# The u blocks of a gated mixer as seven products of half-width matmuls

## The chip, the cores and the metric

The kernel runs on one core of a Trainium2 chip. The metric is the device time of one execution in microseconds (us): for the kernel before, the median of three runs, 2037.05 us (2037.03 to 2038.43). A core has a matmul engine, TensorE (PE; its loads of the stationary operand are shown as PEld), a vector engine, VectorE (DVE), ScalarE for activation functions (ACT), GpSimd (POOL) and SyncE (SP). SP and POOL issue the DMAs.

## The reference

Two layers act on x of 512 tokens by 1024 features, float32. Each layer is a SwiGLU half step, a mixer and a second SwiGLU half step, each with a layer norm behind it. The change is in the mixer's input projection, in the part called u:

```
zq, zf, zi, zg, zu, zv, za, zb = jnp.split(x @ w_in, IN_SPLITS, axis=-1)
...
u = jax.nn.gelu(zu)
v = layer_norm(jax.nn.gelu(zv), sg_ln_g, sg_ln_b)
...
mixed = jnp.einsum('gts,bnsgc->bntgc', ws, v) + sg_bs.T[None, None, :, :, None]
y_b = (u * mixed.reshape(B, T, SG_WIDTH)) @ w_branch_b
```

zu has 512 features, that is, 4 blocks of 128; the sum behind each runs over 1024 features, that is, 8 row tiles of 128.

## The kernel before, in words

**Split operands.** Every large product is made in three terms. An operand is split into a high part (copied by ACT with rounding to the matmul's float32 form, line 126) and a low part (the difference, DVE, line 127), and high x high, high x low and low x high are summed in PSUM.

**Plain blocks.** features(name) takes the next block of w_in from the iterator blk: weights() issues one DMA of 512 KB into a "raw" buffer (line 132, SP's queue) and splits it into two "w" buffers; proj() (line 155) runs 8 row tiles x 3 terms = 24 matmuls of 128 x 128 weights against 512 tokens into one PSUM bank. There are 4 raw buffers (NRAW), 10 w buffers (NW) and 3 "sa" buffers for evictions (NSA).

**Seven products.** Several stages use a scheme for a 2 x 2 product of blocks with seven products instead of eight. In the first product of the SwiGLU (seven_pairs, matmuls at line 590) a unit is a pair of features j and j + 11 of both halves of the weights; tokens and the summed rows are each cut in two halves. The operands of the seven products are, by ORDER: a, t, c, b, a, d, c on the weights' side, where t = a + b, b = d + b, a = a + b and c = a + c are formed in the raw buffers by DVE (sum(), line 570) before the split, and A11, s1, A12, s3, s2, s4, A22 on the side of x. The sums s1 to s4 of x are made by x_sums(). One product is 2 blocks x 4 row tiles x 3 terms = 24 matmuls against 256 tokens, so a pair has 168. PairWeights loads a, b, c and d (two DMAs of 256 KB each), and the split of a weight is written AHEAD = 3 products before its use. The results lie in four banks, A, B, C and E; evictions() takes them out and combines them behind each product.

i and v of the mixer use another form of the scheme (class Seven, two_tokens, matmuls at line 366): there the sums of the weights are formed in DRAM by accumulating DMAs on POOL's queue (sums_in_dram, line 307), and two_b(k), two_c(k), two_d(k) load and split them. two_b(k) makes the weights B11 and t1 (one split), and for even k those of t2 for two k (another split).

**Order of the mixer.** The queries and gates f and q of four heads; the g blocks, four calls of features() with a Sigmoid on ACT (line 1050) and a product on DVE (line 1051) behind each; the u blocks, four calls of features() with a GELU behind each (line 1063); then i and v by two_tokens(); then the gates z and what follows. x_sums (s_task) and sums_in_dram (in_dram) are side tasks, and so are the scores of each head (head_scores: small matmuls sp, lv, lx at lines 892, 953, 963, with DVE work between them) and the outputs of the heads. A hand-written planner (class Flow) keeps a clock of estimated PE time; each tick of a proj() or product() adds the estimated cost, and writes at most one step of a side task that has come due into the program at that place. flow.finish(task) writes all that is left of a task.

**Order of the instructions.** The order on each engine is laid down when the program is built, by the order in which instructions are written and the estimated readiness of their inputs and buffers. An instruction passed through pin() while pinned[0] is true stays behind the one written before it on its engine; the others may be placed earlier or later. seven_pairs() and the loads, sums and splits of its weights are written under pinned[0]; the matmuls themselves, features(), two_tokens() and head_scores() are not.

Of the kernel before, what the change touches and what calls it, by code (L numbers as in the profile page):

```python
# [28 lines left out]
F32 = mybir.dt.float32  # L29
F32R = mybir.dt.float32r  # L30
I32 = mybir.dt.int32
AF = mybir.ActivationFunctionType
ALU = mybir.AluOpType
AX = mybir.AxisListType

P = 128
D = 1024
T = 512
DEPTH = 2
DFF = 2816  # L40
NF = DFF // P
# [42 lines left out]
def trunk(ctx: ExitStack, tc, x_in, xt_in, w13, w2, w_in, w_iv, w_br, w_out, ln_g, ln_b, lb_in, hgn, sgg, sgb, sgws,  # L84
          sgbs, masks, tril_in, ident_in, out):
    nc = tc.nc
    V, S, G, PE = nc.vector, nc.scalar, nc.gpsimd, nc.tensor
# [3 lines left out]
    wk = ctx.enter_context(tc.tile_pool(name="wk", bufs=1))  # L91
# [11 lines left out]
    def slot(name, dtype=F32):  # L103
        return big.tile([P, 2, 512], dtype, tag="h", name=name, bufs=NS)
# [13 lines left out]
    pinned = [False]  # L118

    def pin(ins):  # L120

        if pinned[0]:
            tc.keep_in_program_order(ins)
# [21 lines left out]
    NS, NRAW, NSA = 34, 4, 3  # L145
# [130 lines left out]
    NH2 = NF // 2  # L276
# [257 lines left out]
    AHEAD = 3  # L534

    class PairWeights:
# [25 lines left out]
        def split(self):  # L562
# [2 lines left out]
            split(hi, lo, getattr(self, src))  # L565
            self.parts.append((hi, lo))

        def sum(self, to, u, v):
            to, u, v = (getattr(self, n) for n in (to, u, v))
            pin(V.tensor_tensor(to, u, v, op=ALU.add))  # L570

    def seven_pairs(seven, s, ks, weights_of, first, due):


        half = slice(0, 256), slice(256, 512)
        movs = {"A11": lambda m: (xh[m // 2][:, m % 2, half[0]], xl[m // 2][:, m % 2, half[0]]),
                "A12": lambda m: (xh[2 + m // 2][:, m % 2, half[0]], xl[2 + m // 2][:, m % 2, half[0]]),
                "A22": lambda m: (xh[2 + m // 2][:, m % 2, half[1]], xl[2 + m // 2][:, m % 2, half[1]])}
        for c in s:
            movs[c] = lambda m, c=c: (s[c][0][:, m], s[c][1][:, m])  # L580

        def product(ps, units, c, first):
            for z in range(2):
                hi, lo = units[0][:, z], units[1][:, z]
                for m in range(4):
                    ms = slice(m * P, (m + 1) * P)
                    mh, ml = movs[c](m)
                    for i, (a, v) in enumerate(((hi, mh), (hi, ml), (lo, mh))):
                        start = first and z == 0 and m == 0 and i == 0
                        PE.matmul(ps[:, half[z]], a[:, ms], v, start=start, stop=(m == 3 and i == 2),  # L590
                                  skip_group_check=not (first and z == 0))
                    flow.tick(3 * 120.0)

        pws = {ks[0]: first}
        at = lambda n: (ks[n // 7], n % 7)
        last = 7 * len(ks)
        banks = {}

        def evictions(k, m):
            b, r = banks[k], seven.room(k).rearrange("p q t -> p (q t)")  # L600
            lower, upper = r[:, 0:512], r[:, 512:1024]
            if m == 0:
                pin(S.activation(upper, b["A"], AF.Copy))
            elif m == 2:
                pin(S.activation(lower, b["A"], AF.Silu))
            elif m == 1:
                b["b1"] = wk.tile([P, T], F32, tag="sa", name="b1", bufs=NSA)
                pin(S.activation(b["b1"], b["C"], AF.Copy))
            elif m == 3:
                pin(V.tensor_tensor(b["b1"], b["b1"], b["E"], op=ALU.subtract))  # L610
            elif m == 4:
                pin(V.tensor_tensor(upper, upper, b["B"], op=ALU.subtract))
                pin(V.tensor_tensor(b["b1"], b["b1"], upper, op=ALU.subtract))
            elif m == 5:
                b0 = wk.tile([P, T], F32, tag="sa", name="b0", bufs=NSA)
                pin(V.tensor_tensor(b0, b["C"], upper, op=ALU.subtract))
                pin(V.tensor_tensor(lower, lower, b0, op=ALU.mult))
            elif m == 6:
                pin(V.tensor_tensor(upper, b["E"], upper, op=ALU.add))
                yield  # L620
                pin(S.activation(upper, upper, AF.Silu))
                pin(V.tensor_tensor(upper, upper, b["b1"], op=ALU.mult))

        for n in range(last):
            k, m = at(n)
            nk = at(n + 7)[0] if n + 7 < last else None
            if m == 0 and nk is not None:
                pws[nk] = weights_of(nk)
                pws[nk].load_d()
            elif m == 1 and nk is not None:  # L630
                pws[nk].load_c()
            ev = evictions(*at(n - 1)) if n else iter(())
            next(ev, None)
            if m == 0:
                banks[k] = {c: bank(f"f{c}{k}") for c in "ABCE"}
                pws[k].sum("a", "a", "b")
            elif m == 1:
                pws[k].sum("c", "a", "c")
            elif m == 2 and nk is not None:
                pws[nk].sum("t", "a", "b")  # L640
            elif m == 3 and nk is not None:
                pws[nk].sum("b", "d", "b")
            if n + AHEAD < last:
                pws[at(n + AHEAD)[0]].split()
            for _ in ev:
                pass
            if m == 3:
                for v in due.get(k, ()):
                    seven.activation_sums(v)
            c, mov, _ = ORDER[m]  # L650
            product(banks[k][c], pws[k].parts[m], mov, c == "B" or m in (0, 1, 3))
        for _ in evictions(*at(last - 1)):
            pass

    FRONT = [10]
# [6 lines left out]
    def ffn(l, i, first, next_weights):  # L662
        last = next_weights is None

        front = FRONT
        by_seven = [k for k in range(NH2) if k not in front]
        order = by_seven[0:2] + front + by_seven[2:]
        seven = Seven(lambda k: w2[l, i, k], order, front + by_seven[3:5])
# [26 lines left out]
        s = {}  # L695
        bufs = []
# [4 lines left out]
        def first_weights():  # L701
            pinned[0] = True
            bufs.extend(slot(f"r{v}") for v in ("t", "c0", "c1"))
            pw = weights_of(by_seven[0])
            pw.load_c()
            pw.load_d()
            pw.sum("t", "a", "b")
            for _ in range(AHEAD):
                pw.split()
            pw.sum("b", "d", "b")  # L710
            pinned[0] = False
            return pw

        if first is None:
# [8 lines left out]
            pw = first_weights()  # L723
            plain(js[1], second)
        else:
            first = [blocks(j, w) for j, w in zip(js, first)]
# [5 lines left out]
            for z, j in enumerate(js):  # L732
                pair_of(j, first[z], 256, 256)
                glu(j, first[z])
                if z == 0:
                    pw = first_weights()
        flow.finish(s_task)
        seven.home[by_seven[2]] = (xl[0][:, 0, 256:512], xl[0][:, 1, 256:512], xh[0][:, :, 256:512], xh[1][:, :, 256:512])

        hold = small("hold")  # L740
# [1 line left out]
                                                 op0=ALU.mult, op1=ALU.add))  # L742
        in_dram = flow.add(seven.sums_in_dram(order))
        pinned[0] = True
        seven_pairs(seven, s, by_seven, weights_of, pw, dict(zip((1, 2, 4, 5, 7, 8), ([v] for v in front + by_seven[0:5]))))
        pinned[0] = False
        flow.finish(in_dram)
        return seven.run(0.5 / ALPHA, (l, 2 * i), last, by_seven[5:], next_weights)
# [24 lines left out]

    T_AT = {2: 0, 4: 256, 8: 384, 16: 448, 32: 480, 64: 496, 128: 504}

    def mixer_weights(l):
        return [weights(w_in[l, b], f"{'fq'[b % 2]}{b // 2}", True) for b in range(4)]

    def mixer(l, lb, om, first, next_weights):
# [4 lines left out]
        hg = wk.tile([P, NH], F32, tag="hg", name="hg", bufs=1)  # L784
        nc.gpsimd.dma_start(hg, hgn[l])

        blk = iter(range(4, 32))
        s = {}
        seven = Seven(lambda k: w_iv[l, k], list(range(KT // 2)), [])

        def features(name):
            w = weights(w_in[l, next(blk)], name)
            ps = bank(name)
            proj(ps, w, 0, from_x)
            return ps

        def two_tokens():

            ks, ops, mm = seven.order, seven.ops, seven.mm
# [7 lines left out]
            A, B, C = ([bank(f"{v}{tt}") for tt in range(2)] for v in ("iA", "iB", "iC"))  # L807
            u, p5 = (wk.tile([P, 2, 512], F32, tag="rs", name=v, bufs=2) for v in ("iu", "ip5"))
            for i, k in enumerate(ks):
                seven.two_b(k)  # L810
                if i < len(ks) - 2:
                    for ps, p in ((A, P1), (B, P6), (C, P5)):
                        for tt in range(2):
                            mm(ps, p, [k], tt, True, True)
# [35 lines left out]
        gate, qk, raw, sc = [], [], [], []  # L850
# [194 lines left out]

        gs = [slot(f"gs{i}") for i in range(2)]
        for h in range(NH):
            ps = features(f"g{h}")
            sl = gs[h // 2][:, h % 2, :]
            S.activation(sl, ps, AF.Sigmoid)  # L1050
            V.scalar_tensor_tensor(sl, ps, hg[:, h:h + 1], sl, op0=ALU.mult, op1=ALU.mult)
# [5 lines left out]
                yield from head_out(h)  # L1057


        u = [slot(f"u{i}") for i in range(2)]  # L1060
        for j in range(4):
            ps = features(f"u{j}")
            S.activation(u[j // 2][:, j % 2, :], ps, AF.Gelu_apprx_tanh)
        flow.finish(s_task)
        flow.finish(in_dram)
        two_tokens()
        late.append(flow.add(all_out(), 4000.0))
        cst = slot("cst")
# [39 lines left out]
        z = [[], []]  # L1108
# [177 lines left out]
```

## Time and profile before

| | |
|---|---|
| median of 3 runs | 2037.05 us (2037.03 to 2038.43) |
| profiled execution, time | 2035.33 us |
| profiled execution, span | 2033.5 us |
| mean granted TensorE clock | 0.998 of full |
| busy: PE, PEld | 2022.2, 1840.6 us |
| busy: DVE, ACT, POOL | 1639.4, 996.8, 370.5 us |
| u blocks, layer 0 | from 430.1 to 453.2 us of the span |
| u blocks, layer 1 | from 1440.7 to 1463.8 us of the span |

The profile is one execution on the chip. Busy times are sums over an engine's instructions; "idle before" in the groups and timelines is the time in which the engine had nothing running, with what ended it. Matmuls overlap each other, so the distance between starts, not the duration, is the pace. Names such as u<-xh,h_u give the tile written and the tiles read; L155 is line 155 of the kernel.

### The profile page before, as it was taken

The numbers are of one execution on the slowest core, as the hardware profiler recorded it, in microseconds if no ns is written. First come the engines' busy times: TensorE is split into PE (matmuls) and PEld (weight loads), VectorE is DVE, ScalarE is ACT, GpSimd is POOL, SyncE is SP. The second block draws the span as 40 slices with busy tenths as digits, with TensorE's granted clock in tenths as the row PEclk, the third lists the DMA queues.
The fourth block names the chain that finished last, engine by engine and source line by source line (L and its number), as shares of the span: only waits on it lengthen the run. The fifth ranks groups of instructions, "written<-read, shape, count | busy, mean of one in ns | idle before, by whom it ended". The sixth has DMA issues, their size and how long they took to land. (4 is left out here: it accounts for less than half of the span.)

```text
span 2033.5 us, 33362 instructions
## 1 busy us (share of the span) xinstructions
PE 2022.2 (99%) x12880; PEld 1840.6 (91%) x12880; DVE 1639.4 (81%) x2453; ACT 996.8 (49%) x1438; POOL 370.5 (18%) x478
## 2 busy tenths in 40 slices
PE   9999999999999999999999999999999999999998
PEld 8999988888888999998899999898888889999986
DVE  8999988956436799999789999889564467999986
ACT  6544665336323554556555456662353235444563
POOL 2322002301000143210132320032010002323101
PEclk9999999999999999999999999999999999999999
DMA  6999777735243289988649997776352433999873
GB/s 233 257 258 238 239 253 238 153 110 181 83 154 115 105 234 241 226 258 269 203 153 271 253 243 242 256 231 137 118 175 83 145 114 113 255 239 230 264 258 129
DMA packets 167550, 404.60 MB, mean 199 GB/s; under 512 B 18880, under 2 KB 19008, under 8 KB 167392
## 3 DMA queue, kind: packets, MB, share of 16 engines
q1 hardware_dynamic: 113472, 261.22, 38.2%
q0 software_dynamic: 53920, 141.26, 29.5%
q8 instruction: 101, 1.65, 0.3%
q14 instruction: 57, 0.47, 0.1%
HBM read 380.38 MB, written 131.07 MB: 252 GB/s over the span
## 5 line engine op out<-in xcount | busy, mean ns | idle before, releaser
L307 POOL DMA_DIRECT2D t<-in_w_dram x176 | 145.5, 901 | 219.5 <-DMA t<-in_w_dram 103.1
L127 DVE TENSOR_TENSOR l_pc<-rc,h_pc 128x1024 fp32r<-128x1024 f32 x80 | 97.8, 1222 | 19.0 <-ACT h_pc L126 19.0
L307 POOL DMA_DIRECT2D t<-t x104 | 56.7, 545 | 288.2 <-DMA t<-in_w_dram 258.6
L155 PE MATMUL z<-xh,h_z 128*128 128x512 f32 x256 | 103.2, 403 | 0.0
L155 PE MATMUL z<-xh,l_z 128*128 128x512 f32 x256 | 99.9, 390 | 0.0
L155 PE MATMUL z<-xl,h_z 128*128 128x512 f32 x256 | 99.9, 390 | 0.0
L127 DVE TENSOR_TENSOR l_pa<-ra,h_pa 128x1024 fp32r<-128x1024 f32 x80 | 97.7, 1221 | 0.0
L126 ACT ACTIVATE h_pc<-rc 128x1024 fp32r<-128x1024 f32 x80 | 84.0, 1050 | 21.0 <-PE fB L590 20.0
L186 POOL TENSOR_SCALAR rstd<-ssq 128x1 f32<-128x1 f32 x24 | 19.3, 803 | 406.8 <-ACT sq L211 406.8
L590 PE MATMUL fA<-xh,h_pc 128*128 128x256 f32 x320 | 90.8, 284 | 0.1
L590 PE MATMUL fC<-xs1h,l_pt 128*128 128x256 f32 x320 | 90.7, 283 | 0.0
L590 PE MATMUL fB<-xs2l,h_pa 128*128 128x256 f32 x320 | 90.7, 283 | 0.0
L590 PE MATMUL fC<-xs1l,h_pt 128*128 128x256 f32 x320 | 90.7, 283 | 0.0
L590 PE MATMUL fB<-xs2h,h_pa 128*128 128x256 f32 x320 | 90.7, 283 | 0.0
L590 PE MATMUL fC<-xs4l,h_pd 128*128 128x256 f32 x320 | 90.7, 283 | 0.0
L590 PE MATMUL fE<-xs3l,h_pb 128*128 128x256 f32 x320 | 90.7, 283 | 0.0
L590 PE MATMUL fB<-xs2h,l_pa 128*128 128x256 f32 x320 | 90.7, 283 | 0.0
L590 PE MATMUL fE<-xh,l_pc 128*128 128x256 f32 x320 | 90.7, 283 | 0.0
L590 PE MATMUL fA<-xh,l_pa 128*128 128x256 f32 x320 | 90.7, 283 | 0.0
L590 PE MATMUL fC<-xs4h,l_pd 128*128 128x256 f32 x320 | 90.7, 283 | 0.0
L590 PE MATMUL fE<-xs3h,l_pb 128*128 128x256 f32 x320 | 90.7, 283 | 0.0
L590 PE MATMUL fC<-xs4h,h_pd 128*128 128x256 f32 x320 | 90.7, 283 | 0.0
(411 smaller groups left out, 7561.6 us busy)
## 6 DMA issues: line engine op xcount, KB each, us to landing
t<-in_w_dram POOLq DMA_DIRECT2D x88, 512.0 KB, 8.8
t<-t POOLq DMA_DIRECT2D x104, 256.0 KB, 5.5
r_d<-t SPq DMA_DIRECT2D x104, 256.0 KB, 4.2
t<-in_w_dram POOLq DMA_DIRECT2D x88, 256.0 KB, 7.1
r_c<-in_w_dram SPq DMA_DIRECT2D x44, 512.0 KB, 4.8
ra<-in_w_dram SPq DMA_DIRECT2D x80, 256.0 KB, 6.0
rb<-in_w_dram SPq DMA_DIRECT2D x80, 256.0 KB, 7.2
rc<-in_w_dram SPq DMA_DIRECT2D x80, 256.0 KB, 7.7
```

Of the source, the lines that this page charges most:

```text
L126: pin(S.activation(hi, src, AF.Copy))
L127: pin(V.tensor_tensor(lo, src, hi.bitcast(F32), op=ALU.subtract))
L155: PE.matmul(ps[:, n0:n0 + n], a[:, cs], m[:, n0:n0 + n], start=(i == 0), stop=(i == 3 * nk - 1))
L186: G.tensor_scalar(r, ssq, inv, eps, op0=ALU.mult, op1=ALU.add)
L307: tc.keep_in_program_order(nc.gpsimd.dma_start(*of(k), **kw))
L590: PE.matmul(ps[:, half[z]], a[:, ms], v, start=start, stop=(m == 3 and i == 2), skip_group_check=not (first and z == 0))
```

## The change

The four calls of features() for u are replaced by one pair of the seven-product scheme: seven_pairs() runs with one unit whose a and b are the blocks 0, 1 and 2, 3 of u for the first half of the rows, and c and d the same blocks for the second half. For this seven_pairs() no longer holds the SwiGLU's evictions and its work beside the products, but takes both as functions (evict, beside); the SwiGLU passes what it had. The opening of a first pair (loads of c and d, t = a + b, three splits, b = d + b) becomes PairWeights.begin(). In the mixer, the weights are loaded and begin() is written, pinned, before the weights of the third g block. The side tasks s_task and in_dram are finished before the u blocks instead of behind them. evict_u() takes two copies, four GELUs on ACT and five operations on DVE from the four banks. Beside products 4 and 5 the weights of i and v for k = 0 and 1 are loaded and split, pinned; two_tokens() leaves out what is there. t, a and b take raw buffers, c and d two buffers of tag "rs".

```diff
+        def begin(self):
+            self.load_c()
+            self.load_d()
+            self.sum("t", "a", "b")
+            for _ in range(AHEAD):
+                self.split()
+            self.sum("b", "d", "b")
...
-    def seven_pairs(seven, s, ks, weights_of, first, due):
+    def seven_pairs(s, ks, weights_of, first, evict, beside):
...
-            if m == 3:
-                for v in due.get(k, ()):
-                    seven.activation_sums(v)
+            beside(k, m)
...
+    U_AT = 12
...
-        blk = iter(range(4, 32))
+        blk = iter([*range(4, U_AT), *range(U_AT + 4, 32)])
...
             for i, k in enumerate(ks):
-                seven.two_b(k)
+                if ("B11", k) not in ops:
+                    seven.two_b(k)
...
         for h in range(NH):
+            if h == 2:
+                pinned[0] = True
+                t, c = (wk.tile([P, 2, 512], F32, tag=v, name=f"ru{v}", bufs=n) for v, n in (("raw", NRAW), ("rs", 2)))
+                pw = PairWeights(lambda j: w_in[l, U_AT + 2 * (j // NF) + j % NF // NH2], 0, t, c)
+                pw.begin()
+                pinned[0] = False
             ps = features(f"g{h}")
...
-        u = [slot(f"u{i}") for i in range(2)]
-        for j in range(4):
-            ps = features(f"u{j}")
-            S.activation(u[j // 2][:, j % 2, :], ps, AF.Gelu_apprx_tanh)
         flow.finish(s_task)
         flow.finish(in_dram)
+        u = [slot(f"u{i}") for i in range(2)]
+
+        def evict_u(k, m, b):
+
+            def gelu(i, half, v):
+                pin(S.activation(u[i][:, :, 256 * half:256 * half + 256], v.rearrange("p (z t) -> p z t", z=2),
+                                 AF.Gelu_apprx_tanh))
+
+            if m == 0:
+                b["u"] = wk.tile([P, T], F32, tag="sa", name="uu", bufs=NSA)
+                pin(S.activation(b["u"], b["A"], AF.Copy))
+            elif m == 1:
+                b["b1"] = wk.tile([P, T], F32, tag="sa", name="ub1", bufs=NSA)
+                pin(S.activation(b["b1"], b["C"], AF.Copy))
+            elif m == 2:
+                gelu(0, 0, b["A"])
+            elif m == 3:
+                pin(V.tensor_tensor(b["b1"], b["b1"], b["E"], op=ALU.subtract))
+            elif m == 4:
+                pin(V.tensor_tensor(b["u"], b["u"], b["B"], op=ALU.subtract))
+                pin(V.tensor_tensor(b["b1"], b["b1"], b["u"], op=ALU.subtract))
+                yield
+                gelu(1, 1, b["b1"])
+            elif m == 5:
+                b0 = wk.tile([P, T], F32, tag="sa", name="ub0", bufs=NSA)
+                pin(V.tensor_tensor(b0, b["C"], b["u"], op=ALU.subtract))
+                yield
+                gelu(1, 0, b0)
+            elif m == 6:
+                pin(V.tensor_tensor(b["u"], b["E"], b["u"], op=ALU.add))
+                yield
+                gelu(0, 1, b["u"])
+
+        def next_blocks(k, m):
+            if m in (4, 5):
+                seven.two_b(seven.order[m - 4])
+
+        pinned[0] = True
+        seven_pairs(s, [0], None, pw, evict_u, next_blocks)
+        pinned[0] = False
         two_tokens()
```

More of the change, by code (lines that the diff above doesn't have):

```diff
@@ L597, in seven_pairs @@
         banks = {}
[L599 to L622, printed above, removed]
         for n in range(last):
@@ L631, in seven_pairs @@
                 pws[nk].load_c()
-            ev = evictions(*at(n - 1)) if n else iter(())
+            ev = evict(*at(n - 1), banks[at(n - 1)[0]]) if n else iter(())
             next(ev, None)
@@ L646, in seven_pairs @@
                 pass
-            if m == 3:
-                for v in due.get(k, ()):
-                    seven.activation_sums(v)
+            beside(k, m)
             c, mov, _ = ORDER[m]
             product(banks[k][c], pws[k].parts[m], mov, c == "B" or m in (0, 1, 3))
-        for _ in evictions(*at(last - 1)):
+        for _ in evict(*at(last - 1), banks[at(last - 1)[0]]):
             pass
@@ L704, in first_weights @@
             pw = weights_of(by_seven[0])
[L705 to L710, printed above, removed]
+            pw.begin()
             pinned[0] = False
@@ L737, in ffn, with evictions, sums_of @@
         flow.finish(s_task)
+        due = dict(zip((1, 2, 4, 5, 7, 8), front + by_seven[0:5]))
+        def evictions(k, m, b):
+            r = seven.room(k).rearrange("p q t -> p (q t)")
+            lower, upper = r[:, 0:512], r[:, 512:1024]
+            if m == 0:
+                pin(S.activation(upper, b["A"], AF.Copy))
+            elif m == 2:
+                pin(S.activation(lower, b["A"], AF.Silu))
+            elif m == 1:
+                b["b1"] = wk.tile([P, T], F32, tag="sa", name="b1", bufs=NSA)
+                pin(S.activation(b["b1"], b["C"], AF.Copy))
+            elif m == 3:
+                pin(V.tensor_tensor(b["b1"], b["b1"], b["E"], op=ALU.subtract))
+            elif m == 4:
+                pin(V.tensor_tensor(upper, upper, b["B"], op=ALU.subtract))
+                pin(V.tensor_tensor(b["b1"], b["b1"], upper, op=ALU.subtract))
+            elif m == 5:
+                b0 = wk.tile([P, T], F32, tag="sa", name="b0", bufs=NSA)
+                pin(V.tensor_tensor(b0, b["C"], upper, op=ALU.subtract))
+                pin(V.tensor_tensor(lower, lower, b0, op=ALU.mult))
+            elif m == 6:
+                pin(V.tensor_tensor(upper, b["E"], upper, op=ALU.add))
+                yield
+                pin(S.activation(upper, upper, AF.Silu))
+                pin(V.tensor_tensor(upper, upper, b["b1"], op=ALU.mult))
+        def sums_of(k, m):
+            if m == 3 and k in due:
+                seven.activation_sums(due[k])
         seven.home[by_seven[2]] = (xl[0][:, 0, 256:512], xl[0][:, 1, 256:512], xh[0][:, :, 256:512], xh[1][:, :, 256:512])
@@ L744, in ffn @@
         pinned[0] = True
-        seven_pairs(seven, s, by_seven, weights_of, pw, dict(zip((1, 2, 4, 5, 7, 8), ([v] for v in front + by_seven[0:5]))))
+        seven_pairs(s, by_seven, weights_of, pw, evictions, sums_of)
         pinned[0] = False
@@ L1047, in mixer @@
         for h in range(NH):
+            if h == 2:
+                pinned[0] = True
+                t, c = (wk.tile([P, 2, 512], F32, tag=v, name=f"ru{v}", bufs=n) for v, n in (("raw", NRAW), ("rs", 2)))
+                pw = PairWeights(lambda j: w_in[l, U_AT + 2 * (j // NF) + j % NF // NH2], 0, t, c)
+                pw.begin()
+                pinned[0] = False
             ps = features(f"g{h}")
@@ L1057, in all_out @@
                 yield from head_out(h)
-        u = [slot(f"u{i}") for i in range(2)]
-        for j in range(4):
-            ps = features(f"u{j}")
-            S.activation(u[j // 2][:, j % 2, :], ps, AF.Gelu_apprx_tanh)
         flow.finish(s_task)
         flow.finish(in_dram)
+        u = [slot(f"u{i}") for i in range(2)]
[3 more added lines that the diff above has]
+                                 AF.Gelu_apprx_tanh))
+            if m == 0:
+                b["u"] = wk.tile([P, T], F32, tag="sa", name="uu", bufs=NSA)
+                pin(S.activation(b["u"], b["A"], AF.Copy))
+            elif m == 1:
+                b["b1"] = wk.tile([P, T], F32, tag="sa", name="ub1", bufs=NSA)
+                pin(S.activation(b["b1"], b["C"], AF.Copy))
+            elif m == 2:
+                gelu(0, 0, b["A"])
+            elif m == 3:
+                pin(V.tensor_tensor(b["b1"], b["b1"], b["E"], op=ALU.subtract))
+            elif m == 4:
+                pin(V.tensor_tensor(b["u"], b["u"], b["B"], op=ALU.subtract))
+                pin(V.tensor_tensor(b["b1"], b["b1"], b["u"], op=ALU.subtract))
+                yield
+                gelu(1, 1, b["b1"])
+            elif m == 5:
+                b0 = wk.tile([P, T], F32, tag="sa", name="ub0", bufs=NSA)
+                pin(V.tensor_tensor(b0, b["C"], b["u"], op=ALU.subtract))
+                yield
+                gelu(1, 0, b0)
+            elif m == 6:
+                pin(V.tensor_tensor(b["u"], b["E"], b["u"], op=ALU.add))
+                yield
+                gelu(0, 1, b["u"])
[5 more added lines that the diff above has]
+        pinned[0] = False
         two_tokens()
```

## The prediction

> **What bounds the kernel now.** I read the page first: who is busy, and for how much of the span.
>
> ```profile
> span 2033.5 us, 33362 instructions
> PE 2022.2 (99%) x12880; PEld 1840.6 (91%) x12880; DVE 1639.4 (81%) x2453; ACT 996.8 (49%) x1438; POOL 370.5 (18%) x478
> ```
>
> TensorE (PE) leaves 11.3 us of the span unfilled. A busy PE isn't yet a PE at its pace, so the timeline of PE comes next, at the four blocks of u in layer 0 (columns: start us, duration us; durations overlap, the distance between starts is the pace).
>
> ```profile
> 430.11 0.40 PE L155 MATMUL u<-xh,h_u 128*128 128x512 f32 x1
> ...
> 434.67 0.39 PE L155 MATMUL u<-xh,l_u 128*128 128x512 f32 x1
> 434.99 0.68 PE L953 MATMUL lv<-qk 128*64 128x64 f32 x8
> 435.60 0.50 PE L155 MATMUL u<-xh,h_u 128*128 128x512 f32 x1
> 435.94 0.39 PE L155 MATMUL u<-xl,h_u 128*128 128x512 f32 x1
> ...
> 441.18 0.61 PE L963 MATMUL lx<-qk 128*128 128x128 f32 x4
> ...
> 448.43 0.39 PE L155 MATMUL u<-xh,h_u 128*128 128x512 f32 x1
> ...
> 452.97 0.39 PE L155 MATMUL u<-xh,l_u 128*128 128x512 f32 x1
> 453.19 0.39 PE L366 MATMUL iA<-h_b,xh 128*128 128x512 f32 x1
> ```
>
> From 448.43 to 453.19 there are 21 steps: 4.76/21 = 0.2267 us for each 512-column matmul. The first matmul of i follows the last of u at 453.19 - 452.97 = 0.22 us, the same pace: the boundary at which the change gets its weights ready earlier has no wait to remove. The stage lasts 453.19 - 430.11 = 23.08 us: 96 x 0.2267 = 21.76, and 1.32 for the two inserts (lv, lx) of the last head's scores and the slower step after each.
>
> Then the pace of the form that u gets, in the first SwiGLU:
>
> ```profile
> 46.53 0.28 PE L590 MATMUL fE<-xh,h_pc 128*128 128x256 f32 x1
> ...
> 49.41 0.28 PE L590 MATMUL fA<-xh,h_pa 128*128 128x256 f32 x1
> ```
>
> One product is 24 matmuls (2 blocks, 4 row tiles, 3 terms), and 49.41 - 46.53 = 2.88 us: 0.1200 us each. Last, the busy times by stretch: the end of the g blocks, the u stage, and one pair of the second SwiGLU (columns: stretch, length, PE, PEld, DVE, ACT and POOL busy with counts, granted clock, DMA share, GB/s).
>
> ```profile
> 418.50:430.10 11.60, 11.60 (x61) 9.94 (x60) 9.11 (x19) 2.76 (x6) 0.00 (x0) 1.00 0.51 176
> 430.10:453.20 23.10, 23.10 (x110) 18.94 (x109) 7.31 (x10) 8.51 (x12) 0.59 (x1) 1.00 0.28 94
> 715.00:735.10 20.10, 20.10 (x170) 20.10 (x169) 20.03 (x22) 10.85 (x14) 11.99 (x7) 1.00 0.79 211
> ```
>
> The u stage is PE's alone, with VectorE (DVE) at 7.31 of 23.10 us. In the pair, weight loads (PEld) fill all 20.10 us, and DVE 20.03, yet PE doesn't wait: 170 matmuls are the 168 of a pair and those cut at the ends.
>
> **The matmuls.** Removed: 4 blocks x 8 row tiles x 3 terms = 96 at 0.2267, 21.76 us a layer. Added: 7 x 24 = 168 at 0.1200, 20.16 us. The columns streamed fall by an eighth, the time by 7.4%: 1.60 us a layer, 3.2 us in two. All of this is on PE, which sets the end. [...]
>
> **The inserts.** How score matmuls cost among 256-column ones isn't in the trace; the nearest row is a transposition among half-width matmuls.
>
> ```profile
> 344.80 0.28 PE L155 MATMUL f<-xh,l_f 128*128 128x256 f32 x1
> 344.92 0.60 PE L176 MATMUL tr<-ident,x 128*128 128x128 f32 x4
> 345.27 0.36 PE L155 MATMUL f<-xh,h_f 128*128 128x256 f32 x1
> ```
>
> It adds 345.27 - 344.80 - 0.12 = 0.35 us for 4. In the u stage lv adds 435.60 - 434.67 - 0.23 = 0.70 for 8, about as much each. So I take no change; the ends are a gain of 0.3 a layer (the slower steps behind the inserts vanish) and a loss of 0.3.
>
> **Work ahead of u.** begin() now runs before the weights of g2: three splits and two sums, in written order behind g1's gate. The DVE timeline there, and what a sum and an eviction take:
>
> ```profile
> 418.47 0.75 DVE L1051 SCALAR_TENSOR_TENSOR gs<-g,hg,gs 128x512 f32<-128x512 f32 x1
> 419.13 3.49 DVE L127 TENSOR_TENSOR l_u<-r_u,h_u 128x1024 fp32r<-128x1024 f32 x3
> ...
> 424.99 0.42 DVE L975 TENSOR_TENSOR qk<-qk,g 128x256 f32<-128x256 f32 x1
> ...
> 426.02 1.22 DVE L127 TENSOR_TENSOR l_u<-r_u,h_u 128x1024 fp32r<-128x1024 f32 x1
> 429.56 0.43 DVE L974 TENSOR_TENSOR qk<-qk,g 128x256 f32<-128x256 f32 x1 [2.32 <-PE lv L953]
> ...
> 432.42 0.74 DVE L1051 SCALAR_TENSOR_TENSOR gs<-g,hg,gs 128x512 f32<-128x512 f32 x1
> L570 DVE TENSOR_TENSOR rt<-ra,rb 128x1024 f32<-128x1024 f32 x40 | 48.9, 1222 | 1.8 <-DMA rb<-in_w_dram 1.8
> L613 DVE TENSOR_TENSOR b<-b,r 128x512 f32<-128x512 f32 x40 | 27.7, 692 | 1.2
> ```
>
> The next score matmul on PE that uses these steps:
>
> ```profile
> 428.71 0.81 PE L953 MATMUL lv<-qk 128*96 128x64 f32 x8
> ```
>
> Four l_u splits go (4 x 1.22 = 4.9 us), five operations come (5 x 1.22 = 6.1): 1.2 more, which the idle 2.32 before 429.56 holds. From 419.13 on, sum t ends at 420.4 and l_pa at 421.6; product 0 needs it at 430.1, so 8.5 us of cover. Behind the chain on DVE wait the last heads' score steps: done at 424.99 + 0.42 = 425.4 for lv at 428.7, so they have 3.3 us of cover for a delay of 1.2. If the cover were gone, each microsecond would cost PE one.
>
> **Work beside u.** Added on DVE: two sums (2.4), four splits (4.9) and five evictions at 0.69 (3.5) to the 7.31 that stay, the i/v splits included: 18.1 in a stage of 23.08 - 1.60 = 21.5 us. The quoted pair carries 20.03 in 20.10 without a stall. ACT gets four splits and two copies on 8.51:
>
> ```profile
> 437.49 1.28 ACT L1063 ACT_TABLE_LOAD   x1
> 438.79 0.60 ACT L1063 ACTIVATE u<-u 128x512 f32<-128x512 f32 x1
> ...
> 442.33 1.06 ACT L126 ACTIVATE h_b<-r_b 128x1024 fp32r<-128x1024 f32 x1
> 443.30 0.58 ACT L1063 ACTIVATE u<-u 128x512 f32<-128x512 f32 x1
> ```
>
> That is 8.51 + 4 x 1.06 + 2 x 0.60 = 14.0, and copies between GELUs need no further table load (none lies between 442.33 and 443.30). The last split, c for product 6, is written behind the GELU of product 2, which ends at 430.1 + 3 x 2.88 = 438.7: with table load, GELU and both halves of the split 438.7 + 1.3 + 0.6 + 1.06 + 1.22 = 442.9, needed at 430.1 + 6 x 2.88 = 447.4 (inserts move both): 4.5 us of cover. The earlier splits wait for no eviction by DVE. Cost: nothing; if DVE fell 4.5 us behind, product 6 would wait for the rest.
>
> **Loads and queues.** SP's queue, POOL's DMAs that u now stands behind, and u's loads (count, size, us to landing):
>
> ```profile
> 349.39 65.39 SPq L132 DMA_DIRECT2D r_u<-in_w_in_dram  x4
> 420.41 0.33 SPq L378 DMA_DIRECT2D r_b<-in_w_iv_dram  x1
> 385.42 3.38 POOL L307 DMA_DIRECT2D t<-in_w_iv_dram  x4 [0.44 <-DMA t<-t]
> r_u<-in_w_in_dram SPq DMA_DIRECT2D x4, 512.0 KB, 3.3
> ```
>
> The bytes of u's weights stay (2 MB, as eight DMAs of 256 KB instead of four of 512), and are issued ahead of g2's and g3's loads, which they push back. A load lands in 3.3 us, while SP takes 65 us to issue four, since it waits for buffers; that is the cover. With a and b holding two of the four raw buffers until product 1, g3's load waits for g1's buffer, about as u's second load did. finish(in_dram) moves nothing: its last POOL issue is at 385.42, before u in either order.
>
> **First weights of i and v.** Before, they are ahead already:
>
> ```profile
> 431.27 1.23 DVE L127 TENSOR_TENSOR l_b<-r_b,h_b 128x1024 fp32r<-128x1024 f32 x1 [0.95 <-ACT h_b L126]
> 437.51 1.23 DVE L127 TENSOR_TENSOR l_t<-r_t,h_t 128x1024 fp32r<-128x1024 f32 x1 [1.04 <-ACT h_t L126]
> 443.43 1.23 DVE L127 TENSOR_TENSOR l_b<-r_b,h_b 128x1024 fp32r<-128x1024 f32 x1 [0.85 <-ACT h_b L126]
> ```
>
> Now they come in written order behind the evictions: product 3 ends near 442.9, 0.69 and two splits later it is 446.0; product 4 ends near 445.8, two evictions and the third split later it is 448.4. i begins near 451.6 and needs the third after 18 matmuls, at 455.7. Cover 5.6 and 7.3 us; gain none, cost none.
>
> **Sum.** Span 2033.5 - 3.2 = 2030.3; the profiled run takes 2035.33, 1.83 outside its span, so 2032.1; it lies 1.72 below the median of 2037.05, so I forecast **2033.85 us**, a change of 0.16%. About 0.2% (4.1 us) is what a measurement of this kernel tells from no change.
>
> **Rivals.**
> 1. Slower: begin's chain lands late on DVE. For it: 9.11 of 11.60 us busy there, and written order only forbids it to come early. If it runs behind g3's gate (432.42 + 0.74), l_pa ends at 433.16 + 2.44 = 435.6, product 0 waits 5.5 us, less 1.6 saved: +3.9 a layer, **2044.9**. It decides once l_pa is later than 431.7. Against: its inputs are loaded early, and 2.32 us are free. Chance 0.08.
> 2. Given back: a wait of about 1.6 us a layer, at a score matmul behind the fuller DVE or at the second i/v weight: **2037**. For it: DVE goes from 7.31 to 18.1 us. Against: the pair at 20.03. Chance 0.13.
> 3. More: the matmuls' pace follows their columns, half of 0.2267. Then 168 x 0.1134 = 19.04, 2.7 a layer, **2031.6**. [...] Against: PEld full at 0.1200 in the pair. Chance 0.06.
> 4. Weight loads, 168 for 96, stop overlapping among the score matmuls and evictions of the mixer.
>
> ```profile
> L590 PEld LDWEIGHTS fA<-xh,h_pc 128*128 128x128 f32 x320 | 61.5, 192 | 0.3 <-ACT r L603 0.3
> ```
>
> At a load's own 0.192 us, 168 x 0.192 = 32.3, less 21.8: 10.5 more a layer, **2058**. [...] Against: the same code holds 0.1200 in the SwiGLU. Chance 0.01.
>
> **How the numbers follow.** The forecast has 0.72, with its own range 2032.5 to 2035.2 (the runs shown scatter over 1.4 us). The range over the cases, 2031.5 to 2037.6, takes in rivals 2 and 3 and leaves out 1 and 4. Faster by over 0.2% (under 2033.0): rival 3 and the lower edge of the forecast's scatter, 0.06 + 0.09 = 0.15. Slower: rivals 1 and 4, 0.09. The rest, 0.76, is within 0.2%: most of the forecast, and rival 2.
>
> **What would show it.** Right: u's matmuls at 0.120 us, the stage near 21.5 us in both layers, the first of i 0.12 to 0.23 us behind the last of u, l_pa done by 422, PE's idle time still near 11 us. Wrong: a gap on PE before product 0 or before a score matmul with DVE as its releaser (rivals 1, 2), or a pace other than 0.120 (3, 4).

## The result, and the profile after

The changed kernel takes 2048.16 us (median of six runs, 2046.36 to 2049.82), the kernel before 2037.04 (median of six, 2034.38 to 2038.43). The ratio is 1.0057, with a 95% interval of 1.0044 to 1.0070: slower by 11.1 us, where 3.2 less had been forecast. The profiled execution after took 2048.17 us. Its page begins:

```profile
span 2046.4 us, 33700 instructions
PE 2023.0 (99%) x13024; PEld 1848.6 (90%) x13024; DVE 1661.1 (81%) x2477; ACT 1004.6 (49%) x1448; POOL 370.0 (18%) x478
```

PE is unfilled for 2046.4 - 2023.0 = 23.4 us, where it had been 11.3. The view of waits says where (PE after; columns: engine, line and tile, what it waited for, us in total, times, longest us):

```profile
PE g L155 <- ACT h_g L126: 11.8, 2, 5.9
PE idle L1205 <- DVE zero L1202: 1.1, 1, 1.1
PE g L155 <- DVE l_g L127: 0.5, 2, 0.3
```

The first row is new, once in each layer. It isn't in the u stage: it is a g block, ahead of u, that waits for the high part of its weights. (The four g blocks are g0 to g3 here; this one is g2.) The timeline of PE after, from the score step before that block to the first of i in layer 0:

```profile
414.25 0.68 PE L966 MATMUL lv<-qk 128*64 128x64 f32 x8
420.82 0.80 PE L155 MATMUL g<-xh,h_g 128*128 128x512 f32 x1 [5.89 <-ACT h_g L126]
421.41 0.63 PE L155 MATMUL g<-xl,h_g 128*128 128x512 f32 x1
...
423.59 0.80 PE L155 MATMUL g<-xh,l_g 128*128 128x512 f32 x1 [0.27 <-DVE l_g L127]
424.19 0.63 PE L155 MATMUL g<-xh,h_g 128*128 128x512 f32 x1
424.61 0.63 PE L155 MATMUL g<-xl,h_g 128*128 128x512 f32 x1
425.04 0.63 PE L155 MATMUL g<-xh,l_g 128*128 128x512 f32 x1
...
426.25 0.40 PE L155 MATMUL g<-xh,l_g 128*128 128x512 f32 x1
426.49 0.39 PE L155 MATMUL g<-xh,h_g 128*128 128x512 f32 x1
...
437.21 0.28 PE L600 MATMUL fA<-xh,h_pa 128*128 128x256 f32 x1
...
458.48 0.28 PE L600 MATMUL fE<-xh,l_pc 128*128 128x256 f32 x1
458.60 0.40 PE L366 MATMUL iA<-h_b,xh 128*128 128x512 f32 x1
```

Two things are to be read here. The u stage is what was forecast: 458.60 - 437.21 = 21.39 us for 23.08 before, 1.69 less. And the way to it is longer. The same score step before, as the timeline of PE before has it:

```profile
415.97 0.68 PE L953 MATMUL lv<-qk 128*64 128x64 f32 x8
```

From there to the first of u it was 430.11 - 415.97 = 14.14 us; now it is 437.21 - 414.25 = 22.96, or 8.82 more: 5.89 and 0.27 of waits, and 2.66 for matmuls that start 0.42 to 0.43 us apart after the wait (424.19, 424.61, 425.04), in place of 0.23, until about 426.25. So layer 0 costs 8.82 - 1.69 = 7.13 us more. Layer 1 has the same two waits, but the slow matmuls end sooner: there the way to u takes 1454.93 - 1432.41 = 22.52 us for 1440.71 - 1426.57 = 14.14 before, and the layer costs 8.38 - 1.69 = 6.69 more. Together that is 13.8 us. The changed kernel's profile was 415.97 - 414.25 = 1.72 us ahead when it came to this place in layer 0, which leaves 12.1 of the 12.9 us between the spans; the other 0.8 lies outside these stages. (The profile before lay 1.71 us below its median, that after at its own; hence 11.1 between the medians.)

The windows of the changed kernel (columns as in the prediction) show the stage ahead of u, with the granted clock at 0.85, and the u stage:

```profile
414.90:437.20 22.30, 16.14 (x69) 13.24 (x69) 13.90 (x25) 6.73 (x11) 0.00 (x0) 0.85 0.23 71
437.20:458.60 21.40, 21.40 (x182) 21.18 (x181) 15.97 (x20) 12.81 (x17) 0.59 (x1) 1.00 0.33 104
```

Why was h_g late? ACT's timeline after, and the one SP row that holds the loads of g2 and g3 (g2's issued at 394.58, g3's at the row's end, 394.58 + 25.91 = 420.5):

```profile
414.36 0.60 ACT L1069 ACTIVATE gs<-g 128x512 f32<-128x512 f32 x1 [4.90 <-PE g L155]
...
415.24 1.04 ACT L126 ACTIVATE h_pa<-ra 128x1024 fp32r<-128x1024 f32 x1
417.81 1.06 ACT L126 ACTIVATE h_pt<-ruraw 128x1024 fp32r<-128x1024 f32 x1 [1.53 <-DVE ruraw L579]
418.78 1.04 ACT L126 ACTIVATE h_pc<-rurs 128x1024 fp32r<-128x1024 f32 x1
419.72 1.04 ACT L126 ACTIVATE h_g<-r_g 128x1024 fp32r<-128x1024 f32 x1
...
423.32 1.06 ACT L126 ACTIVATE h_g<-r_g 128x1024 fp32r<-128x1024 f32 x1 [2.56 <-DMA r_g<-in_w_in_dram]
```

```profile
394.58 25.91 SPq L132 DMA_DIRECT2D r_g<-in_w_in_dram  x2
```

g2's data were asked for at 394.58 and a load of these lands in 3.8 us (the page's median for r_g), yet ACT splits them at 419.72, right behind begin()'s three splits, which are pinned behind g1's gate (the Sigmoid at 414.36), and it had stood idle for 4.90 us ahead of that gate. PE ends g1 at the same time as the gate starts, and so waits for the gate, the sum t and three splits that it doesn't need yet. The 0.27 us come from DVE, where g2's low part stands behind begin()'s second sum:

```profile
421.18 1.22 DVE L579 TENSOR_TENSOR rb<-rd,rb 128x1024 f32<-128x1024 f32 x1
422.32 1.22 DVE L127 TENSOR_TENSOR l_g<-r_g,h_g 128x1024 fp32r<-128x1024 f32 x1
```

In the kernel before, ACT made g2's h_g long before g1's gate:

```profile
395.01 1.05 ACT L126 ACTIVATE h_g<-r_g 128x1024 fp32r<-128x1024 f32 x1
...
416.08 0.60 ACT L1050 ACTIVATE gs<-g 128x512 f32<-128x512 f32 x1 [3.81 <-PE g L155]
```

### The profile page after: what moved, and what is told of

Its sections match the earlier page's. It is cut to its first block, busy times and chain, and to the rows that moved or that the text cites. A ratio compares the mean times of both kernels' runs of the same rounds, so it can differ in the third digit from the quotient of the medians.

```text
span 2046.4 us, 33700 instructions
## 1 busy us (share of the span) xinstructions
PE 2023.0 (99%) x13024; PEld 1848.6 (90%) x13024; DVE 1661.1 (81%) x2477; ACT 1004.6 (49%) x1448; POOL 370.0 (18%) x478
## 5 line engine op out<-in xcount | busy, mean ns | idle before, releaser
L127 DVE TENSOR_TENSOR l_pa<-ra,h_pa 128x1024 fp32r<-128x1024 f32 x84 | 102.4, 1218 | 0.0
L600 PE MATMUL fA<-xh,h_pc 128*128 128x256 f32 x336 | 95.2, 283 | 0.1
L600 PE MATMUL fC<-xs1h,h_pt 128*128 128x256 f32 x336 | 95.3, 284 | 0.0
L600 PE MATMUL fE<-xs3h,h_pb 128*128 128x256 f32 x336 | 95.2, 283 | 0.0
L600 PE MATMUL fB<-xs2h,h_pa 128*128 128x256 f32 x336 | 95.1, 283 | 0.0
L600 PE MATMUL fB<-xs2l,h_pa 128*128 128x256 f32 x336 | 95.1, 283 | 0.0
L600 PE MATMUL fE<-xh,h_pc 128*128 128x256 f32 x336 | 95.1, 283 | 0.0
L600 PE MATMUL fE<-xl,h_pc 128*128 128x256 f32 x336 | 95.1, 283 | 0.0
L600 PE MATMUL fA<-xl,h_pc 128*128 128x256 f32 x336 | 95.1, 283 | 0.0
L600 PE MATMUL fA<-xh,l_pc 128*128 128x256 f32 x336 | 95.1, 283 | 0.0
```

Of the source, the lines that this page charges most:

```text
L127: pin(V.tensor_tensor(lo, src, hi.bitcast(F32), op=ALU.subtract))
```

## The experiments

The theory: the product form gains what was forecast, and the loss is wholly that begin() is written ahead of the weights of g2 and g3, so that their splits are laid behind begin()'s own. Rivals: the pin alone makes it; the raw buffer that t takes makes it; the products themselves do.

**Weights of g2 and g3 written first (e1).** Relative to the changed kernel:

```diff
-        def features(name):
-            w = weights(w_in[l, next(blk)], name)
+        def features(name, w=None):
+            w = w or weights(w_in[l, next(blk)], name)
...
+        early = {}
         for h in range(NH):
             if h == 2:
+                early = {v: weights(w_in[l, next(blk)], f"g{v}") for v in (2, 3)}
                 pinned[0] = True
...
-            ps = features(f"g{h}")
+            ps = features(f"g{h}", early.get(h))
```

> The weights of g2 and g3 are loaded and split in the text ahead of begin(), all else as after the change. Theory A (written order: g2's split is laid behind begin's three splits on ScalarE, which wait for g1's gate): the wait of PE before g2 (5.9 us a layer) and the slow matmuls behind it vanish, u keeps its 21.4 us, so 1.6 to 1.7 us a layer less than before the change: about 2033.7 us. Theory B (raw buffers held by t, a and b): vanishes too, 2033.7. Theory C (VectorE has too much work there, wherever it stands): a wait of 2 us or more a layer stays, before product 0 or a score matmul, 2037 or more.

Measured: 2030.7 us against 2034.5 for the kernel before on the same chip, ratio 0.9982 (0.9973 to 0.9991). The wait is gone from PE's list, ACT makes the two splits at 392.69 and 406.77 again, and a split of begin() floats in behind them (timelines of ACT and PE, layer 0):

```profile
392.69 1.05 ACT L126 ACTIVATE h_g<-r_g 128x1024 fp32r<-128x1024 f32 x1
...
406.77 1.05 ACT L126 ACTIVATE h_g<-r_g 128x1024 fp32r<-128x1024 f32 x1
408.86 1.06 ACT L126 ACTIVATE h_pa<-ra 128x1024 fp32r<-128x1024 f32 x1
```

```profile
413.63 0.68 PE L966 MATMUL lv<-qk 128*64 128x64 f32 x8
...
427.77 0.29 PE L600 MATMUL fA<-xh,h_pa 128*128 128x256 f32 x1
...
449.15 0.40 PE L366 MATMUL iA<-h_b,xh 128*128 128x512 f32 x1
```

From the score step to u it is 427.77 - 413.63 = 14.14 us, to the hundredth what it was before the change, and the stage takes 449.15 - 427.77 = 21.38. The order of a few lines of the program is the whole loss, and without it the forecast gain is there: 3.8 us by the medians, 2 x 1.70 by the stages. This version beats both kernels. The expected times of e1 to e4 are reckoned from the 2037 us of the kernel before as it was first measured; beside these runs it took 2034.5, so the ratios are what compares: 2033.7 of 2037.05 is 0.9984. Theories A and B expected the same here, so e1 speaks against C but doesn't decide between them; e4, e9 and e10 take that up.

**Only g2's weights first (e2).** As e1, with g2 alone in `early`.

> Only g2's weights ahead of begin(); g3's stay behind it. Theory A: g2's wait vanishes; g3's split comes at about the time it had after the change (near 421 to 424 in layer 0), when PE reaches g3 near 424 of a span without the wait, so PE waits 0 to 1.5 us before g3: 2033.7 to 2037. Theory B: g3's load waits for t's raw buffer until 420 and lands at 423.3: the same. Theory C: 2037 or more.

Measured: 2035.7 us, ratio 1.0007 (0.9998 to 1.0016). g2's wait is gone, but another stands in its place (PE's waits, and the row in layer 0):

```profile
PE lv L966 <- DVE qk L958: 3.1, 2, 1.5
```

```profile
424.22 0.86 PE L966 MATMUL lv<-qk 128*96 128x64 f32 x8 [1.54 <-DVE qk L958]
424.89 0.36 PE L600 MATMUL fA<-xh,h_pa 128*128 128x256 f32 x1
```

g3's split on DVE now comes behind begin()'s chain, at 424.98; the order on PE fills in with matmuls of product 0, which stand ahead of g3's, and a score step waits 1.54 us for DVE. Both blocks have to be ahead. The two waits are 3.1 of the 5.0 us by which this is slower than e1; from the first of g to the first of i a layer takes 53.87 us for 52.13 in e1, 3.5 us in two layers, and the rest lies outside these stages. The ratio is above the expected 0.9984 to 1.0000. After this shorter wait PE's pace is 0.12 us a step in product 0 and 0.23 in g3, at a granted clock of 1.00 from 414.90 to 437.20.

**begin() at its place, unpinned (e3).** The changed kernel without `pinned[0] = True` ahead of begin().

> begin() at its place, but not pinned: its sum and splits may be laid ahead of g1's gate. Theory A, in the form that the pin behind g1's gate makes begin late and all that is written behind it too: the wait before g2 shrinks to 0 to 3 us a layer, 2034 to 2041. Theory A, in the form that written order alone decides (five operations of VectorE ahead of g2's split, pinned or not): 4 us or more a layer stay, 2043 or more. Theory B: t takes its raw buffer as before; the wait stays at 5.9 us, 2048.

Measured: 2060.41 us, ratio 1.0125 (1.0111 to 1.0139): none of the outcomes fits whole. The waits of the g blocks fall from 12.3 to 7.6 us, and a larger one comes up some 65 us earlier, at the start of the mixer, where DVE is held by a sum whose load hasn't landed (PE's waits, then DVE):

```profile
PE f L155 <- DVE xl L127: 11.8, 2, 6.3
PE g L155 <- DVE l_g L127: 4.8, 2, 2.4
PE g L155 <- ACT h_g L126: 2.8, 2, 1.4
```

```profile
354.72 1.23 DVE L579 TENSOR_TENSOR rb<-rd,rb 128x1024 f32<-128x1024 f32 x1 [4.21 <-DMA rd<-in_w_in_dram]
355.86 1.63 DVE L127 TENSOR_TENSOR xl<-tr,xh 128x256 fp32r<-128x256 f32 x4
```

Freed of the pin, the sums move up to where their buffers are free, onto a DVE on which PE depends at the mixer's start; and g2's split is behind begin()'s splits as before (h_g at 422.67). So the pin isn't the cause; at this place it kept a worse wait away.

**t in a large buffer instead of a raw one (e4).** The changed kernel with

```diff
-                t, c = (wk.tile([P, 2, 512], F32, tag=v, name=f"ru{v}", bufs=n) for v, n in (("raw", NRAW), ("rs", 2)))
+                t, c = slot("ruraw"), wk.tile([P, 2, 512], F32, tag="rs", name="rurs", bufs=2)
```

> The sum t takes a buffer of the large pool instead of a raw buffer, so the raw buffer that t held until its split (420.1 us in layer 0) is free for a load of g2 or g3. Theory A: the loads come earlier, but g2's split stays behind begin's on ScalarE: PE's wait before g2 stays near 5.9 us a layer, 2046 to 2049. Theory B: the wait goes, 2034 to 2038.

Measured: 2047.78 us, ratio 1.0066 (1.0054 to 1.0079), and the first row of PE's waits is word for word that of the changed kernel. Yet the loads have moved (SP, ACT):

```profile
348.44 46.69 SPq L132 DMA_DIRECT2D r_g<-in_w_in_dram  x2
```

```profile
419.95 1.99 ACT L126 ACTIVATE h_g<-r_g 128x1024 fp32r<-128x1024 f32 x2
```

Both loads are issued by 348.44 + 46.69 = 395.1, and ACT still splits both blocks at 419.95, behind h_pc. By the same 3.8 us, an estimate from the changed kernel's page, the data lay there for over 20; neither the load nor t's raw buffer alone is the cause.

**The kernel before, with plain u blocks loaded and split early (e5).** Nothing of the seven products; only the order of begin():

```diff
-        blk = iter(range(4, 32))
+        blk = iter([*range(4, 12), *range(15, 32)])
...
+            if h == 2:
+                pinned[0] = True
+                early = [weights(w_in[l, 12 + j], f"u{j}") for j in range(3)]
+                pinned[0] = False
...
-            ps = features(f"u{j}")
+            ps = features(f"u{j}", early.pop(0) if early else None)
```

> The kernel before, with plain u blocks; only the loads and splits of the first three u blocks are written, pinned, ahead of g2's weights, where the change wrote begin(). No seven products, no sums. Theory A (written order): g2's split is laid behind the three pinned splits, which stand behind g1's gate; PE waits 4 to 5 us before g2 in each layer and then runs slow matmuls for 4 to 5 us: 11 to 14 us more than the kernel before, ratio 1.0055 to 1.007. Rival D (the loss needs the products: their sums, raw buffers held to product 1, or their evictions): ratio within 0.998 to 1.002.

Measured: 2049.72 us, ratio 1.0073 (1.0061 to 1.0086), a little above what was expected. Order alone, without one product, makes the wait (PE and ACT):

```profile
419.00 0.79 PE L155 MATMUL g<-xh,h_g 128*128 128x512 f32 x1 [4.25 <-ACT h_g L126]
```

```profile
417.90 1.04 ACT L126 ACTIVATE h_g<-r_g 128x1024 fp32r<-128x1024 f32 x1
```

Here the gain of 1.7 us a layer is missing, so that a shorter wait gives a like loss; the slow pace behind the wait is there too, 0.43 us a step up to 424.12.

**e1 without the weights of i and v beside products 4 and 5 (e6).** next_blocks() does nothing; two_tokens() loads and splits all.

> As e1_g23_first (weights of g2 and g3 ahead of begin), without the loads and splits of the first i and v weights beside products 4 and 5: they are written in two_tokens() again. The prediction's step (they are ahead anyway, gain none, cost none): the same as e1_g23_first, ratio 0.998 within 0.0008. Rival: i waits for its weights behind the last evictions, 1 us or more a layer, ratio 0.9992 or more.

Measured: 2031.2 us, ratio 0.9982 (0.9973 to 0.9991), as e1. The first of i still follows the last of u at the pace (PE):

```profile
449.54 0.28 PE L600 MATMUL fE<-xh,l_pc 128*128 128x256 f32 x1
449.66 0.40 PE L366 MATMUL iA<-h_b,xh 128*128 128x512 f32 x1
```

That part of the change gains nothing and costs nothing.

**e1 with begin() unpinned (e8).**

> As e1_g23_first, with begin() not pinned. If written order behind g2's and g3's weights is what matters, the pin costs and brings nothing: ratio 0.998 within 0.0008, no wait of PE over 1 us in the mixer. If the pin is what keeps begin()'s sums from standing on VectorE ahead of other work whose inputs come sooner (as in the run where begin() was not pinned and stood ahead of g2's weights), waits of some us come back: ratio 1.001 or more.

Measured: 2031.19 us, ratio 0.9982 (0.9973 to 0.9991), again as e1. Written behind g2 and g3, begin() needs no pin; the wait of e3 came from its place together with the missing pin.

**The changed order, with t and begin()'s splits in buffers of their own (e9).** If the claim on buffers is what ties g2's split to begin()'s, buffers from the large pool should free it, with the program's order as the change has it:

```diff
+        big = False
...
+            if self.big and len(self.parts) < AHEAD:
+                hi, lo = (slot(f"{v}_p{src}_{self.k}", F32R) for v in "hl")
+            else:
                 hi, lo = (wk.tile([P, 2, 512], F32R, tag="w", name=f"{v}_p{src}_{self.k}", bufs=NW) for v in "hl")
...
+                t, c = slot("ruraw"), wk.tile([P, 2, 512], F32, tag="rs", name="rurs", bufs=2)
...
+                pw.big = True
```

> The text of the change in its order (begin() written and pinned ahead of g2's weights), but t and the three splits of begin() take buffers of the large pool, so that g2's raw and w buffers aren't claimed behind theirs. If the wait before g2 comes from buffers claimed in written order (g2's load and split are laid behind the first writers of t and of begin's w buffers), it goes, and the ratio is that of e1_g23_first, 0.998 within 0.001. If written order acts by itself, whatever the buffers, the wait of about 5.9 us a layer stays: 1.005 to 1.007.

Measured: 2037.67 us, ratio 1.0017 (1.0008 to 1.0026). The waits for h_g and l_g are gone from PE's list, from the score step at 413.67 to u at 427.81 it is 14.14 us as in the kernel before, and ACT splits g2 and g3 early:

```profile
392.74 1.05 ACT L126 ACTIVATE h_g<-r_g 128x1024 fp32r<-128x1024 f32 x1
...
406.81 1.05 ACT L126 ACTIVATE h_g<-r_g 128x1024 fp32r<-128x1024 f32 x1
```

But the time of e1 isn't reached, for the borrowed buffers bring a wait of their own (PE's waits, then DVE):

```profile
PE fE L605 <- DVE gs L1076: 4.0, 2, 2.0
```

```profile
430.83 1.23 DVE L127 TENSOR_TENSOR l_pt<-ruraw,h_pt 128x1024 fp32r<-128x1024 f32 x1 [2.81 <-PE fA L605]
...
435.55 1.41 DVE L1076 SCALAR_TENSOR_TENSOR gs<-g,hg,gs 128x512 f32<-128x512 f32 x2 [0.55 <-ACT gs L1075]
```

The second split of begin() on DVE, l_pt, doesn't start before 430.83 and waits for a product on PE, and the gates of g2 and g3, which stand behind it, come at 435.55. The u stage takes 24.13 us for the 21.38 of e1. The expected time was missed; what was expected of g2's wait came about. Which borrowed buffer held l_pt was not tried.

**Only the splits in buffers of their own, t in a raw one (e10).** As e9 without the line of t.

> Only the three splits of begin() take buffers of the large pool; t stays in a raw buffer. If g2's raw buffer, too, is claimed behind t's, whose first writer is the sum on VectorE behind g1's gate, g2's split is laid behind that sum: PE waits 3.5 to 5.5 us a layer, ratio 1.003 to 1.006. If the w buffers alone were the cause, the wait goes: 0.998 within 0.001.

Measured: 2053.6 us, ratio 1.0096 (1.0082 to 1.0110), more than expected. g2's split is late again, now right behind the first reader of t, and a new wait comes to it (ACT, then PE's waits):

```profile
418.17 1.06 ACT L126 ACTIVATE h_pt<-ruraw 128x1024 fp32r<-128x1024 f32 x1 [1.53 <-DVE ruraw L584]
419.14 1.04 ACT L126 ACTIVATE h_g<-r_g 128x1024 fp32r<-128x1024 f32 x1
```

```profile
PE g L155 <- ACT h_g L126: 9.9, 2, 4.9
PE fE L605 <- ACT h_pb L126: 4.1, 2, 2.1
```

The u stage grows to 25.22 us, for PE waits 2.06 us in it for h_pb and then runs slow matmuls once more, 0.21 us a step for 0.12. With the changed kernel, e4 and e9 this is a table of two by two: t in a raw buffer or not, begin()'s splits in w buffers or not. g2's split comes early only where begin() takes neither; either claim alone holds it. So the blocks are tied through the pools from which they take buffers in the order of the text. That it is this rule by which the order on ACT is laid, and not some other that goes with the same buffers, is inferred from the four kernels; the choice itself leaves no row in a trace.

## Why the prediction was wrong, step by step

- **The matmuls**: right. 1.69 us a layer for the forecast 1.60, at 0.12 us a step; the stage of e1, where nothing else moves, gains 1.70 a layer.
- **The inserts**: right. 21.39 us are 20.16 and 1.23, for 1.32 before.
- **Work ahead of u**: here the prediction failed. Its own chain was timed well enough: l_pa ended on DVE at 418.9, ahead of the forecast 421.6, and product 0 waited for nothing. The step that fell is "Behind the chain on DVE wait the last heads' score steps": it asked who waits behind begin() on DVE alone, and only for work that is written far behind. Nearest behind begin() in the text stand the weights of g2, with a split on ACT and one on DVE, and PE needs them the moment g1 ends, when begin() is only being let go by g1's gate. ACT's three splits weren't counted at that place at all. The size could have been had from the profile before: g2's split at 395.01 lies ahead of g1's gate at 416.08, and what is pinned behind that gate and written ahead of g2 puts into g2's way the gate on ACT and DVE, the sum t, and on ACT h_pt, h_pc and its own split: 0.60 + 0.75 + 1.22 + 3 x 1.05 = 5.7 us, for the 5.89 measured. That the two lie so close is partly luck: the sum leaves out 0.94 us of score steps on DVE between the gate's two parts (414.96 to 415.90) and the 0.57 us for which PE still had lv to run, and from the gate's start to the end of g2's split it was 420.76 - 414.36 = 6.40. The slower pace behind the wait (0.42 to 0.43 us a step, 2.66 us in all) was in no row of before.
- **Work beside u**: right in that it cost nothing; busy times were 15.97 us on DVE and 12.81 on ACT, for 18.1 and 14.0 forecast.
- **Loads and queues**: the loads were pushed back as said, but the cover was misjudged, and g3's load waited for t's buffer, not g1's (25.2 us behind l_pt in the waits of SP's queue): its split waited 2.56 us for the data at 423.32. PE didn't wait for it: it came to g3 only at 430.92, and the 0.27 us are g2's low part on DVE. e4, where both loads are early, shows that the loads aren't what counts.
- **First weights of i and v**: right, no gain and no cost (0.12 us between u and i; e6 the same as e1).
- **Rivals.** The first named the right chain, begin() behind a gate, and the right sign; its victim was product 0, its gate g3's, and its price 5.5 us a layer. The wait fell on g2, at 5.89 and 2.66 on top. Rivals 2 to 4 didn't occur: no wait in the u stage, a pace of 0.12.

## What to carry to other kernels

Work that is moved ahead of something must be held against what now stands directly behind it in the text, on each engine that it uses, above all the loads and splits of the next block, which take buffers from the same pools. Write the operands that are needed first, first; moving a few lines was worth 15 us here (ratios 1.0057 and 0.9982), far more than the change itself. To price such a move, look in the old trace for how early the displaced split is made and at which event the new one is released.

## What the hardware showed beside this

After PE had idled for 5.89 us (changed kernel) or 4.25 us (e5), its matmuls of 512 columns started 0.42 to 0.43 us apart, in place of 0.2267, until 5.4 us (layer 0) and 4.5 us (layer 1) after the wait in the changed kernel, and 5.1 us after it in e5 (layer 0); after 1.54 us (e2) they didn't. So in the changed kernel the wait of 5.9 us cost 8.4 to 8.8, with the 0.27 behind it. The mark in the profile is the granted clock: 0.85 in the stretch with the wait (in e5 too), for 1.00 in the next, and 0.50 in each slice of 1 us from 420 to 426. What lowers this clock, and what brings it back, isn't shown.

Behind shorter waits the runs differ. In e10 a wait of 2.06 us in the u stage was followed by matmuls of 256 columns 0.21 us apart, in place of 0.12, from 446.22 to 449.00; the granted clock from 437.20 to 458.60 was 0.92. In e3, waits of 1.41 and 2.42 us with about 1 us of matmuls between them were followed by 0.43 us a step up to 432.53, and the granted clock from 414.90 to 437.20 was 0.85. Yet 2.00 us in e9 left the pace at 0.12, at a granted clock of 1.00 from 437.20 to 458.60. What decides between e9 and e10, the 0.06 us or something else, isn't shown.
